# Row means fused on VectorE, squares alone on ScalarE, and a first load in two pieces: a change to a load, compute, store kernel

## The chip, the cores and the metric

The kernel runs on one core of a Trainium2 chip. The metric is the device time of one execution in microseconds (us). "Span" is the time from the first to the last instruction in a profile; it is some 1.8 us shorter than the time. In the views DVE is VectorE, ACT ScalarE, POOL GpSimd and SP SyncE, the engine that issues the DMAs here; a q after a name is that engine's sequencer. A transfer has landed when its completion is signalled. The "chain" is the profile's own account of the work that ended last, followed back from step to step to what released it.

## The reference

```python
x = np.random.randn(1024, 4096).astype(np.float32)     # axis = -1
mean = np.mean(x, axis=axis, keepdims=True)
return ((x - mean) ** 2).astype(np.float32)
```

16.78 MB are read and as many written; per element there is one addition for the mean, one subtraction, one multiplication.

## The kernel before

The 1024 rows are two tiles of 128 partitions with four whole rows (64 KiB) in each partition. A tile is loaded by one DMA, worked on in place, and stored by one DMA, all issued by SP.

```python
for i in range(ntiles):                       # ntiles = 2
    x_tile = io.tile([P, Q * D], F32)         # P = 128, Q = 4, D = 4096
    nc.sync.dma_start(out=x_tile, in_=x_t[i])
...
for i in range(ntiles):
    row = [tiles[i][:, q * D:(q + 1) * D] for q in range(Q)]
    m3 = mean_on_act(row[3])                  # ScalarE: Identity with accumulator
    m0 = mean_on_dve(row[0])                  # VectorE: reduce_sum, then a scaling of 128x1
    square_on_act(row[3], m3)                 # ScalarE: Square with the bias -mean
    m1 = mean_on_dve(row[1]); square_on_act(row[0], m0)
    m2 = mean_on_dve(row[2]); square_on_act(row[1], m1)
    square_on_act(row[2][:, :H], m2)          # H = 2304 of 4096 columns
    back = row[2][:, H:]
    nc.vector.tensor_scalar_add(out=back, in0=back, scalar1=m2)
    nc.vector.tensor_mul(out=back, in0=back, in1=back)
    nc.sync.dma_start(out=out_t[i], in_=tiles[i])
```

Of the kernel before, what the change touches and what calls it, by code (L numbers as in the profile page):

```python
# [2 lines left out]

os.environ.setdefault("NEURON_RT_ULTRASERVER_MODE", "4")

# [4 lines left out]

F32 = mybir.dt.float32
ACT = mybir.ActivationFunctionType


@with_exitstack
def kernel(
    ctx: ExitStack,
    tc: tile.TileContext,
    x: bass.AP,
    axis: bass.AP,  # L20
    out: bass.AP,
):



    nc = tc.nc

    B, D = x.shape
    P = nc.NUM_PARTITIONS
    Q = 4  # L30
    H = D * 9 // 16
    assert B % (P * Q) == 0
    ntiles = B // (P * Q)
    inv_d = 1.0 / float(D)

    x_t = x.rearrange("(n p q) d -> n p (q d)", p=P, q=Q)
    out_t = out.rearrange("(n p q) d -> n p (q d)", p=P, q=Q)

    io = ctx.enter_context(tc.tile_pool(name="io", bufs=ntiles))
    scratch = ctx.enter_context(tc.tile_pool(name="scratch", bufs=1))  # L40
    stats = ctx.enter_context(tc.tile_pool(name="stats", bufs=2 * ntiles * Q))

    tiles = []
    for i in range(ntiles):
        x_tile = io.tile([P, Q * D], F32)
        nc.sync.dma_start(out=x_tile, in_=x_t[i])  # L46
        tiles.append(x_tile)

    inorder = tc.keep_in_program_order

    def mean_on_act(row):
        copy = scratch.tile([P, D], F32)
        neg_mean = stats.tile([P, 1], F32)
        nc.scalar.activation(  # L54
            out=copy, in_=row, func=ACT.Identity, scale=-inv_d, accum_out=neg_mean
        )
        return neg_mean

    def mean_on_dve(row):
        neg_sum = stats.tile([P, 1], F32)  # L60
        neg_mean = stats.tile([P, 1], F32)
        inorder(nc.vector.reduce_sum(  # L62
            out=neg_sum, in_=row, axis=mybir.AxisListType.X, negate=True
        ))
        inorder(nc.vector.tensor_scalar_mul(out=neg_mean, in0=neg_sum, scalar1=inv_d))  # L65
        return neg_mean

    def square_on_act(part, neg_mean):
        inorder(nc.scalar.activation(  # L69
            out=part, in_=part, func=ACT.Square, bias=neg_mean, scale=1.0  # L70
        ))

    for i in range(ntiles):
        row = [tiles[i][:, q * D:(q + 1) * D] for q in range(Q)]
        m3 = mean_on_act(row[3])
        m0 = mean_on_dve(row[0])
        square_on_act(row[3], m3)
        m1 = mean_on_dve(row[1])
        square_on_act(row[0], m0)
        m2 = mean_on_dve(row[2])  # L80
        square_on_act(row[1], m1)
        square_on_act(row[2][:, :H], m2)
        back = row[2][:, H:]
        nc.vector.tensor_scalar_add(out=back, in0=back, scalar1=m2)  # L84
        nc.vector.tensor_mul(out=back, in0=back, in1=back)  # L85
        nc.sync.dma_start(out=out_t[i], in_=tiles[i])


# [1 line left out]
_INS = ['x', 'axis']  # L90
_OUTS = [((1024, 4096), 'float32')]

_NUMBERS = {'axis': -1}


# [26 lines left out]
```

## Time and profile before

| | before |
|---|---|
| time, median of the first 3 runs | 83.25 us (83.16 to 83.27) |
| span of the profiled run | 81.4 us |
| VectorE, ScalarE busy | 33.4 us, 34.7 us |
| DMA packets, share of 16 engines | 96.0% |
| loads landed | 22.71 and 42.05 us |
| stores issued | 39.68 and 58.96 us |

The busy shares alone say which engine has time to spare. What bounds the kernel is read from the windows between the landings and the issues in the last two rows; the prediction below shows those lines. For the experiments one more view is needed: windows of 2 us around the place where the second load ends and the first store begins. Its columns are those of the windows table in the prediction: busy time of VectorE, ScalarE and GpSimd, the clock, the DMA share, GB/s.

```profile
38.00:40.00 2.00, 1.60 (x1) 1.47 (x1) 0.00 (x0) 1.00 1.21 524
40.00:42.00 2.00, 0.00 (x0) 0.00 (x0) 0.00 (x0) 1.00 1.22 524
```

In each of these windows every one of the 16 DMA engines starts one packet of 64 KiB (524 GB/s in 2 us is 16 of them). A packet is booked whole where it starts, so the DMA share times 2 us is the mean duration of a packet: 1.21 x 2 = 2.42 us for the last packets of the second load, 2.44 for the first of the store.

### The profile page before, as it was taken

The numbers are of one execution on the slowest core, as the hardware profiler recorded it, in microseconds if no ns is written. First come the engines' busy times: TensorE is split into PE (matmuls) and PEld (weight loads), VectorE is DVE, ScalarE is ACT, GpSimd is POOL, SyncE is SP. The second block draws the span as 40 slices with busy tenths as digits, with TensorE's granted clock in tenths as the row PEclk, the third lists the DMA queues.
The fourth block names the chain that finished last, engine by engine and source line by source line (L and its number), as shares of the span: only waits on it lengthen the run. The fifth ranks groups of instructions, "written<-read, shape, count | busy, mean of one in ns | idle before, by whom it ended". The sixth has DMA issues, their size and how long they took to land.

```text
span 81.4 us, 79 instructions
## 1 busy us (share of the span) xinstructions
DVE 33.4 (41%) x16; ACT 34.7 (43%) x13; POOL 0.2 (0%) x4
## 2 busy tenths in 40 slices
DVE  0000000000089999999439999999900000000000
ACT  6000000000089999999339999999800000000000
POOL 0000000000000000000000000000000000000000
DMA  9099956999982999992999992999997499998390
GB/s 483 32 515 515 483 258 290 515 515 515 515 386 129 515 515 515 515 451 129 451 515 515 515 483 129 418 515 515 515 515 322 193 515 515 515 515 386 161 483 0
DMA packets 577, 33.55 MB, mean 412 GB/s; under 512 B 65, under 2 KB 65, under 8 KB 65
## 3 DMA queue, kind: packets, MB, share of 16 engines
q1 hardware_dynamic: 576, 33.55, 96.0%
q14 instruction: 1, 0.00, 0.0%
HBM read 16.78 MB, written 16.78 MB: 412 GB/s over the span
## 4 chain that ended last, share of the span: by engine, by line
DMA 50%; DVE 21%; SPq 0%; issue 0%
DMA x_tile<-in_x_dram 50%; DVE neg_sum L62 16%; DVE x_tile L85 2%; DVE x_tile L84 1%; DVE neg_mean L65 1%; SPq L46 0%
## 5 line engine op out<-in xcount | busy, mean ns | idle before, releaser
L62 DVE TENSOR_REDUCE neg_sum<-x_tile 128x1 f32<-128x4096 f32 x6 | 26.5, 4413 | 25.2 <-DMA x_tile<-in_x_dram 25.2
L69 ACT ACTIVATE x_tile<-x_tile,neg_mean 128x4096 f32<-128x4096 f32 (+1 forms) x8 | 26.0, 3323 | 0.1
L54 ACT ACTIVATE copy<-x_tile 128x4096 f32<-128x4096 f32 x2 | 7.2, 3617 | 23.3 <-DMA x_tile<-in_x_dram 23.3
L85 DVE TENSOR_TENSOR x_tile<-x_tile 128x1792 f32<-128x1792 f32 x2 | 4.1, 2026 | 0.1
L84 DVE TENSOR_SCALAR x_tile<-x_tile,neg_mean 128x1792 f32<-128x1792 f32 x2 | 2.3, 1154 | 0.1
L54 ACT ACT_TABLE_LOAD x1 | 1.3, 1283 | 0.7 <-PEq L103 0.7
L65 DVE TENSOR_SCALAR neg_mean<-neg_sum 128x1 f32<-128x1 f32 x6 | 0.9, 154 | 0.2
L54 ACT ACTIVATION_READ_ACCUMULATOR copy<-x_tile 128x1 f32 x2 | 0.4, 187 | 0.0
L103 POOL MEMSET const-bfloat16-1.0<- 128x1 bf16 x1 | 0.1, 101 | 0.0
L103 POOL MEMSET const-uint8-127<- 128x1 uint8 x1 | 0.1, 101 | 0.0
L103 POOL MEMSET const-float32-0.0<- 128x1 f32 x1 | 0.1, 98 | 0.2 <-issue 0.2
L103 POOL MEMSET const-float32-1.0<- 128x1 f32 x1 | 0.1, 98 | 0.0
## 6 DMA issues: line engine op xcount, KB each, us to landing
x_tile<-in_x_dram SPq DMA_DIRECT2D x2, 31.4
out_dram<-x_tile SPq DMA_DIRECT2D x2, 21.7
```

Source lines behind the costliest of these rows:

```text
L54: nc.scalar.activation(out=copy, in_=row, func=ACT.Identity, scale=-inv_d, accum_out=neg_mean)
L62: inorder(nc.vector.reduce_sum(out=neg_sum, in_=row, axis=mybir.AxisListType.X, negate=True))
L65: inorder(nc.vector.tensor_scalar_mul(out=neg_mean, in0=neg_sum, scalar1=inv_d))
L69: inorder(nc.scalar.activation(out=part, in_=part, func=ACT.Square, bias=neg_mean, scale=1.0))
L84: nc.vector.tensor_scalar_add(out=back, in0=back, scalar1=m2)
L85: nc.vector.tensor_mul(out=back, in0=back, in1=back)
L103: nc = _bacc.Bacc("TRN2", target_bir_lowering=False, num_devices=1)
```

## The change

The intent: take both kinds of mean off the two engines' long instructions. One fused VectorE instruction adds the two halves of a row and sums the result, 2048 pairs where there were 4096 elements; ScalarE has no mean to compute any more and squares nearly everything. The first load is cut so that its first 2 KiB per partition are a transfer of their own.

```diff
+ADD = mybir.AluOpType.add
...
-    H = D * 9 // 16
+    HEAD = 512
+    HALF = D // 2
+    LAST = D - D // 8
...
-        nc.sync.dma_start(out=x_tile, in_=x_t[i])
+        cuts = [0, HEAD, Q * D] if i == 0 else [0, Q * D]
+        for lo, hi in zip(cuts, cuts[1:]):
+            nc.sync.dma_start(out=x_tile[:, lo:hi], in_=x_t[i][:, lo:hi])
... (mean_on_act, mean_on_dve, square_on_act and their calls go)
+        for q in range(Q):
+            row = tiles[i][:, q * D:(q + 1) * D]
+            pairs = scratch.tile([P, HALF], F32)
+            neg_mean = stats.tile([P, 1], F32)
+            inorder(nc.vector.tensor_tensor_reduce(
+                out=pairs, in0=row[:, :HALF], in1=row[:, HALF:],
+                scale=-inv_d, scalar=0.0, op0=ADD, op1=ADD, accum_out=neg_mean,
+            ))
+            cut = D if q < Q - 1 else LAST
+            nc.scalar.activation(
+                out=row[:, :cut], in_=row[:, :cut],
+                func=ACT.Square, bias=neg_mean, scale=1.0,
+            )
+            if cut < D:
+                rest = row[:, cut:]
+                nc.vector.tensor_scalar_add(out=rest, in0=rest, scalar1=neg_mean)
+                nc.vector.tensor_mul(out=rest, in0=rest, in1=rest)
```

More of the change, by code (lines that the diff above doesn't have):

```diff
@@ L40 @@
     scratch = ctx.enter_context(tc.tile_pool(name="scratch", bufs=1))
-    stats = ctx.enter_context(tc.tile_pool(name="stats", bufs=2 * ntiles * Q))
+    stats = ctx.enter_context(tc.tile_pool(name="stats", bufs=ntiles * Q))
     tiles = []
@@ L45 @@
         x_tile = io.tile([P, Q * D], F32)
-        nc.sync.dma_start(out=x_tile, in_=x_t[i])
+        cuts = [0, HEAD, Q * D] if i == 0 else [0, Q * D]
+        for lo, hi in zip(cuts, cuts[1:]):
+            nc.sync.dma_start(out=x_tile[:, lo:hi], in_=x_t[i][:, lo:hi])
         tiles.append(x_tile)
     inorder = tc.keep_in_program_order
-    def mean_on_act(row):
-        copy = scratch.tile([P, D], F32)
-        neg_mean = stats.tile([P, 1], F32)
-        nc.scalar.activation(
-            out=copy, in_=row, func=ACT.Identity, scale=-inv_d, accum_out=neg_mean
-        )
-        return neg_mean
@@ L59, in mean_on_dve @@
-    def mean_on_dve(row):
-        neg_sum = stats.tile([P, 1], F32)
-        neg_mean = stats.tile([P, 1], F32)
-        inorder(nc.vector.reduce_sum(
-            out=neg_sum, in_=row, axis=mybir.AxisListType.X, negate=True
-        ))
-        inorder(nc.vector.tensor_scalar_mul(out=neg_mean, in0=neg_sum, scalar1=inv_d))
-        return neg_mean
-    def square_on_act(part, neg_mean):
-        inorder(nc.scalar.activation(
-            out=part, in_=part, func=ACT.Square, bias=neg_mean, scale=1.0
-        ))
@@ L73 @@
-    for i in range(ntiles):
-        row = [tiles[i][:, q * D:(q + 1) * D] for q in range(Q)]
-        m3 = mean_on_act(row[3])
-        m0 = mean_on_dve(row[0])
-        square_on_act(row[3], m3)
-        m1 = mean_on_dve(row[1])
-        square_on_act(row[0], m0)
-        m2 = mean_on_dve(row[2])
-        square_on_act(row[1], m1)
-        square_on_act(row[2][:, :H], m2)
-        back = row[2][:, H:]
-        nc.vector.tensor_scalar_add(out=back, in0=back, scalar1=m2)
-        nc.vector.tensor_mul(out=back, in0=back, in1=back)
+    for i in range(ntiles):
+        for q in range(Q):
[3 more added lines that the diff above has]
+            inorder(nc.vector.tensor_tensor_reduce(
+                out=pairs,
+                in0=row[:, :HALF],
+                in1=row[:, HALF:],
+                scale=-inv_d,
+                scalar=0.0,
+                op0=ADD,
+                op1=ADD,
+                accum_out=neg_mean,
+            ))
+            cut = D if q < Q - 1 else LAST
+            nc.scalar.activation(
+                out=row[:, :cut],
+                in_=row[:, :cut],
+                func=ACT.Square,
+                bias=neg_mean,
+                scale=1.0,
+            )
[3 more added lines that the diff above has]
+                nc.vector.tensor_mul(out=rest, in0=rest, in1=rest)
```

## The prediction

> **What bounds the kernel now.** I read the page of the kernel before first: busy shares, DMA queues, and the chain that ended last.
>
> ```profile
> span 81.4 us, 79 instructions
> ...
> DVE 33.4 (41%) x16; ACT 34.7 (43%) x13; POOL 0.2 (0%) x4
> ...
> q1 hardware_dynamic: 576, 33.55, 96.0%
> ...
> DMA 50%; DVE 21%; SPq 0%; issue 0%
> ```
>
> VectorE and ScalarE work under half of the span; the packets of the one DMA queue fill 96.0% of the time of its 16 engines. The chain seems to say that VectorE still holds 21% of the way to the end, but its shares sum to 71%: it stops where the second store is issued, and says nothing of what that store found in front of it. So I asked for the windows between the four events that the timeline gives: first load landed (22.71), first store issued (39.68), second load landed (42.05), second store issued (58.96).
>
> ```profile
> core 0: us, DVE busy (x) ACT busy (x) POOL busy (x), PEclk, DMA share, GB/s
> 1.70:22.71 21.01, 0.00 (x0) 0.31 (x1) 0.00 (x0) 1.00 1.07 449
> 22.71:39.68 16.97, 16.71 (x8) 16.72 (x6) 0.00 (x0) 1.00 1.00 433
> 39.68:42.05 2.37, 0.00 (x0) 0.00 (x0) 0.00 (x0) 1.00 1.03 442
> 42.05:58.96 16.91, 16.71 (x8) 16.72 (x6) 0.00 (x0) 1.00 1.00 434
> 58.96:80.30 21.34, 0.00 (x0) 0.00 (x0) 0.00 (x0) 1.00 0.91 393
> ```
>
> The column before the last is the DMA share. It is 1.00 in both stretches of computing: the first is covered by the second load, the second by the first store. (A packet is booked whole at its start, which puts the first row above 1 and the last below it.) From 1.75 us, when packets start, to the last window's end the queue hardly rests: 33.55 MB in 78.6 us is 427 GB/s. What is left outside it is 1.7 us of start and 1.1 us of end in the span, and the 1.85 us between the span (81.4) and the time (83.25).
>
> The second thing to know is how much slack the computing has. The issues of the stores give it:
>
> ```profile
> 39.68 19.67 SPq L86 DMA_DIRECT2D out_dram<-x_tile  x2
> ...
> DMA to landing us min/median/max: 21.6/21.7/21.7
> ```
>
> A store alone needs 8.39 MB / 0.433 = 19.4 us, so of its 21.7 us some 2.3 are waiting behind the transfer in front and the latency at both ends. The first load shows a latency: issued at 0.73, its first packets start at 1.75, 1.0 us later. So the first store was issued at most about 1.3 us before it would leave a hole. **Earlier stores gain next to nothing; stores later by over about a microsecond cost one for one.**
>
> The third view is the DMA rows of three zooms of 1 us in 40 slices (from 1.5, from 4.5 and from 7.0 us), which show when each engine's first, second and third packets start:
>
> ```profile
> DMA  0000000000990099099999000000000090000000
> ...
> DMA  0000000009009090900090999900000090000900
> ...
> DMA  0000009090090900990999000000090000900000
> ```
>
> The first mark moves from 1.75 (slice 10 of 25 ns) to 4.72 to 7.15: the first 64 KiB packet takes 3.0 us, later ones 2.4. So the stream pays about 0.6 us once to get going.
>
> **What the Trainium skill says.** First, "DMA: Bandwidth & Descriptors", section "Where 436 GB/s comes from": the ports give 435.2 GB/s. The windows' 433 and 434 agree; this queue has nothing left. Second, "VectorE: DVE Perf Modes", "The perf-mode tier table": tensor_reduce and fp32 tensor_tensor both run at one element a cycle (0.96 GHz). The rows by form agree:
>
> ```profile
> L62 DVE TENSOR_REDUCE neg_sum<-x_tile 128x1 f32<-128x4096 f32 x6 | 26.5, 4413 | 25.2 <-DMA x_tile<-in_x_dram 25.2
> L69 ACT ACTIVATE x_tile<-x_tile,neg_mean 128x4096 f32<-128x4096 f32 x6 | 21.8, 3698 | 0.1
> L69 ACT ACTIVATE x_tile<-x_tile,neg_mean 128x2304 f32<-128x2304 f32 x2 | 4.4, 2200 | 0.0
> L85 DVE TENSOR_TENSOR x_tile<-x_tile 128x1792 f32<-128x1792 f32 x2 | 4.1, 2026 | 0.1
> ```
>
> 4096/0.96 is 4267 ns of the 4413, and 1792/0.96 is 1867 of the 2026: 1 cycle per element and 146 to 159 ns fixed. The page does not list the fused instruction of the change; that it too takes a pair a cycle is my assumption. Third, "ScalarE: Activation LUTs", "What ACT_TABLE_LOAD costs": about 1283 ns plus 1380 of drain. The trace has the 1283 at 0.73 us, where nothing waits for it. Fourth, "DMA: Bandwidth & Descriptors", "Why small descriptors are slow (HBM only)": a fixed cost of a few cycles per packet. No data packet here is small, but the zoom on the end (78 to 81.4 us) has 16 packets of 4 bytes, one per engine, in 0.3% of the time: 10 ns each.
>
> **The change part by part.**
>
> (a) Means. Removed per tile: three reductions of 4413 with their scalings of 154 ns on VectorE, and on ScalarE one mean of 3617 and a read of its accumulator of 187. Added: four fused instructions over pairs, 2048/0.96 + 159 = 2.29 us each (estimated from the tensor_tensor row), each followed by an accumulator read; with the 0.19 of ScalarE's own read, a mean costs about 2.5 us. VectorE falls from 16.7 to about 4 x 2.5 plus the tail of 512 columns: TENSOR_SCALAR over 1792 took 1154 and TENSOR_TENSOR 2026, so 512 take about 0.49 and 0.69 (1.04 and 0.53 ns less per column dropped), 11.2 us in all, and never in the way, because a mean per 2.5 us outruns a square per 3.6.
>
> (b) Squares. Before, three full rows and 2304 columns, 13.01 us in the timeline (their sum 13.29 less three overlaps of 0.093). Now three full rows and 3584 columns. The slope (3698 - 2200)/1792 is 0.836 ns per column, so 3584 take 3270: 3 x 3.698 + 3.270 - 0.28 = 14.08 us. The first must await the first mean.
>
> (c) The stage. 2.5 + 14.1 + 0.1 to the issue = 16.7 us, against 16.97 now: stores leave **0.3 us earlier**. The order of instructions shows one snag: the table load of ScalarE now carries the waits for the first load, so it runs at about 22.7. 1.28 us hide behind the first mean's 2.5; with the page's drain, 2.66, it would delay the first square by 0.2. So the first store is 0.1 to 0.3 earlier, the second 0.3. Both are hidden by the busy queue. I credit 0.05 us for small holes between the second load and the first store.
>
> (d) The first load. Same bytes; each engine gets eight packets of 2 KiB more and one more semaphore packet, at 10 ns each: +0.09 us, on the path, because the queue is the path. Its third issue costs SP another 0.4 us, but the second part is issued by about 1.6 us, while 16 KiB per engine keep the engines busy from 1.75 until well past 2.3 (16 KiB / 27 GB/s = 0.6, plus the 0.6 of start). It may trim the 0.6 us of start if short packets fill the pipe sooner; I credit 0.1.
>
> Sum: 83.25 - 0.05 + 0.09 - 0.1 = **83.2 us**.
>
> **The rivals.**
> 1. The fused instruction runs at half rate. Then a mean takes 2048 x 2/0.96 + 159 + 190 = 4.6 us, the fourth is ready at 18.5 after landing, its square ends at 21.8, and the first store leaves near 44.5, 4.8 later. Less the slack of about 1.3 there is a hole of 3.5 us: about 86.8. The second stage ends at 63.9, near the end of the delayed first store, so it adds little. For it: nothing in this profile shows the instruction. Against it: the running sum is fed by one result per cycle as the reduction before is.
> 2. The chain is right as it reads, and VectorE's 21% are on the path. Then the saving of the second stage, 0.3 us, is had in full: 82.9. Against it: DMA share 1.00 in that window.
> 3. The start is what the split buys: the whole 0.6 us of the first packet goes, 82.7. For it: somebody cut only the first load. Against it: a read must travel to HBM and back whatever its size, so I think most of it stays.
> 4. The small runs are slow: 256 KiB at half rate, and a late second part, +0.6: 83.8.
>
> **Range and chances.** Rivals 2 to 4 span 82.7 to 83.8 and are all within 1%; the repeats spread over 0.11. I take 82.8 to 83.6 for 8 in 10. Faster by 2% (under 81.6) would need 1.65 us out of a queue that has 0.6 to give: 1%. Slower by 2% (over 84.9) is rival 1 or something like it: 5%. Within 2%: 94%.
>
> **What would show it.** Right: VectorE busy about 22 us and ScalarE about 30, the fused row near 2.3 us, stages of about 16.7 us, DMA share 1.00 while they run, stores landing over 21 us after their issue, and the same span to a few tenths. Step (d) is told by the first packets: if second-round starts stay near 4.7 us, the start was not shortened. Wrong: a fused row of over 4 us; a DMA share well below 1 around 40 to 44 us; a store landing in under 20 us, which would mean that it found the queue empty; or a landing of the first load far from 22.7.

## The result and the profile after

The changed kernel takes 83.22 us (median of 6 runs, 83.05 to 83.58), the kernel before 83.23 (6 runs, 83.16 to 83.27): ratio 1.0004, 95% interval 0.9983 to 1.0024. Here and below a ratio is the mean time of one kernel's runs over that of the other's of the same rounds, so it is not quite the ratio of the medians quoted.

The page of the changed kernel, busy times, queue and chain:

```profile
span 81.5 us, 84 instructions
...
DVE 20.8 (25%) x20; ACT 29.4 (36%) x9; POOL 0.2 (0%) x4
...
q1 hardware_dynamic: 720, 33.55, 95.8%
...
DMA 50%; ACT 13%; ACTq 4%; DVE 3%; SPq 1%; issue 0%
```

VectorE lost 12.6 us of work and ScalarE 5.3, and the span did not move. The chain put VectorE at 21% before; it puts ScalarE and its sequencer at 17% now, and the time is the same. Whether such a share is on the path at all is tested below (e3_no_compute, e11_bare_second). The windows with the same borders as those shown of the kernel before tell why:

```profile
22.71:39.68 16.97, 10.38 (x10) 15.36 (x5) 0.00 (x0) 1.00 1.00 433
...
42.05:58.96 16.91, 10.36 (x10) 14.08 (x4) 0.00 (x0) 1.00 1.00 434
```

The DMA share and the GB/s in both stages of computing are to the digit those of before. The rows by form (elements out and in, count, busy us, mean ns) and then the timeline of the first stage show the new work:

```profile
L61 DVE CUSTOM_DVE_ANT_0 pairs<-x_tile 128x2048 f32<-128x2048 f32 x8 | 18.3, 2291 | 31.7 <-DMA x_tile<-in_x_dram 31.5
L72 ACT ACTIVATE x_tile<-x_tile,neg_mean 128x3584 f32<-128x3584 f32 x2 | 6.5, 3265 | 0.0
L61 DVE DVE_READ_ACCUMULATOR2_ANT neg_mean<- 128x1 f32 x8 | 0.7, 81 | 0.0
```

```profile
22.71 1.28 ACT L72 ACT_TABLE_LOAD   x1 [22.71 <-DMA x_tile<-in_x_dram]
22.76 2.29 DVE L61 CUSTOM_DVE_ANT_0 pairs<-x_tile 128x2048 f32<-128x2048 f32 x1 [22.76 <-DMA x_tile<-in_x_dram]
...
25.10 14.08 ACT L72 ACTIVATE x_tile<-x_tile,neg_mean 128x4096 f32<-128x4096 f32 x4 [1.10 <-DVE neg_mean L61]
...
39.20 19.61 SPq L83 DMA_DIRECT2D out_dram<-x_tile  x2
```

The first load lands where it did (22.71), the fused instruction takes 2291 ns for its 2048 pairs, the table load now stands behind the load but ends 1.1 us before the first mean is there, and the first store goes out at 39.20, 0.48 us earlier than before. That gain does not show in the time.

The spread of the changed kernel (0.53 us against 0.11) was not foreseen. It rests on one run of six, 83.58; the other five lie within 0.22. Later, 11 runs of the kernel before spread over 0.36 and over 0.43 us, so that the changed kernel spreads more is not shown.

### The profile page after: what moved, and what is told of

Read it like the earlier page. It is cut to its first block, busy times and chain, and to the rows that moved or that the text cites. A ratio compares the mean times of both kernels' runs of the same rounds, so it can differ in the third digit from the quotient of the medians.

```text
span 81.5 us, 84 instructions
## 1 busy us (share of the span) xinstructions
DVE 20.8 (25%) x20; ACT 29.4 (36%) x9; POOL 0.2 (0%) x4
## 4 chain that ended last, share of the span: by engine, by line
DMA 50%; ACT 13%; ACTq 4%; DVE 3%; SPq 1%; issue 0%
DMA x_tile<-in_x_dram 50%; ACT x_tile L72 13%; ACTq L114 4%; DVE pairs L61 3%; SPq L52 1%; DVE neg_mean L61 0%
## 5 line engine op out<-in xcount | busy, mean ns | idle before, releaser
L72 ACT ACTIVATE x_tile<-x_tile,neg_mean 128x4096 f32<-128x4096 f32 (+1 forms) x8 | 28.2, 3590 | 6.3 <-DVE neg_mean L61 6.3
L61 DVE CUSTOM_DVE_ANT_0 pairs<-x_tile 128x2048 f32<-128x2048 f32 x8 | 18.3, 2291 | 31.7 <-DMA x_tile<-in_x_dram 31.5
L72 ACT ACT_TABLE_LOAD x1 | 1.3, 1283 | 22.7 <-DMA x_tile<-in_x_dram 22.7
L82 DVE TENSOR_TENSOR x_tile<-x_tile 128x512 f32<-128x512 f32 x2 | 1.4, 692 | 0.1
L81 DVE TENSOR_SCALAR x_tile<-x_tile,neg_mean 128x512 f32<-128x512 f32 x2 | 1.0, 488 | 0.1
L61 DVE DVE_READ_ACCUMULATOR2_ANT neg_mean<- 128x1 f32 x8 | 0.7, 81 | 0.0
```

Of the source, the lines that this page charges most:

```text
L61: inorder(nc.vector.tensor_tensor_reduce(out=pairs, in0=row[:, :HALF], in1=row[:, HALF:], scale=-inv_d, scalar=0.0, op0=ADD, op1=ADD, accu ...
L72: nc.scalar.activation(out=row[:, :cut], in_=row[:, :cut], func=ACT.Square, bias=neg_mean, scale=1.0,)
L81: nc.vector.tensor_scalar_add(out=rest, in0=rest, scalar1=neg_mean)
L82: nc.vector.tensor_mul(out=rest, in0=rest, in1=rest)
```

## The experiments

Twelve kernels ran. Kernels are compared only within the same rounds. The kernel before had a median of 83.16 in the first two calls (11 and 7 runs) and of 83.24 in the third (11 runs).

### The parts of the change, one at a time

**e1_means_only**: the changed kernel with the load left whole.

```diff
-        cuts = [0, HEAD, Q * D] if i == 0 else [0, Q * D]
+        cuts = [0, Q * D]
```

> The change without its split of the first load. Theory (the one DMA queue sets the time, both stages of computing lie behind a transfer): stores still issued 0.3 to 0.5 us earlier than before, time 83.2 us, within 0.15 of both kernels; the spread of the runs as before (0.1). Rival (the chain of the kernel before is right, computing in the second stage is on the path): 0.45 us faster than before, 82.8.

Measured: 83.50 us (83.28 to 83.75, 6 runs), ratio 1.0040 (1.0020 to 1.0059). A miss for both theories: the means alone are neither neutral nor a gain but 0.34 us slower, and their spread is 0.47. Its profiled run took 83.28, so the trace shows its best run.

**e2_split_only**: the kernel before with the split of the first load alone.

```diff
-        nc.sync.dma_start(out=x_tile, in_=x_t[i])
+        cuts = [0, 512, Q * D] if i == 0 else [0, Q * D]
+        for lo, hi in zip(cuts, cuts[1:]):
+            nc.sync.dma_start(out=x_tile[:, lo:hi], in_=x_t[i][:, lo:hi])
```

> The kernel before with the first load split into runs of 2 KiB and 62 KiB, nothing else. Theory (the split moves only packets; it adds some 9 ns per extra packet and does not shorten the start): 83.25 to 83.4 us, first load landing within 0.1 us of 22.7. Rival (the split buys the start, and the change then loses it elsewhere): 82.7 to 83.0. If the wider spread of the changed kernel (83.05 to 83.58) belongs to the split, it shows here and not in the run without the split.

Measured: 83.13 us (83.02 to 83.15, 5 runs), ratio 0.9991 (0.9978 to 1.0004). No gain that could be told from none, and a narrow spread (0.13). The median lies 0.12 under the least that was expected: the price of the extra packets does not show in the time.

### Taking the computing away

**e3_no_compute**: the loop over the rows removed; each tile is stored as it was loaded (wrong, and the comparison with the reference says so).

```diff
-        for q in range(Q):
-            ... (all means and squares)
         nc.sync.dma_start(out=out_t[i], in_=tiles[i])
```

> The changed kernel with all computing taken out: each tile is stored as it was loaded (a wrong result on purpose). The first store can then be issued when the first load lands, 16 us earlier than in the changed kernel. Theory (the queue is full from its first packet to its last): the same time to 0.3 us, 82.9 to 83.3, because 33.55 MB still pass at about 430 GB/s. Rival (the chain that ended last is right: computing is 20% of the way to the end): 17 us less, about 66 us.

Measured: 84.39 us (84.22 to 84.63, 5 runs), ratio 1.0151 (1.0130 to 1.0173). The rival that believes the chain is out by 18 us. But my theory missed too: without any computing the kernel is 1.2 us **slower**. The timeline has the issue, and the 2 us windows have the loss (no compute engines worked, so the columns are GpSimd, clock, DMA share and GB/s):

```profile
22.68 20.82 SPq L57 DMA_DIRECT2D out_dram<-x_tile  x2
```

```profile
38.00:40.00 2.00, 0.00 (x0) 1.00 1.85 524
40.00:42.00 2.00, 0.00 (x0) 1.00 0.00 0
```

The same 16 packets start between 38 and 40 us, the last ones of the second load. Their mean duration is 1.85 x 2 = 3.70 us in place of 2.42: each lasts 1.28 us longer, and no store packet starts before 42. The packets before and after them have their usual length. So the loss sits in one place, the load's last packets, and here the store already waited behind them. From this came the new theory: a store issued *too early* costs time.

### The turn from load to store

**e9_early**: the changed kernel with half of the last row given to VectorE, which has time for it. ScalarE, the later of the two, gets done 1.28 us sooner, and the result is right.

```diff
-    LAST = D - D // 8
+    LAST = D // 2
```

> The changed kernel with half of the last row squared by VectorE, not an eighth: ScalarE has 1536 columns less at the end, 1.28 us, and both stores leave at 37.9 in place of 39.2. The run without computing lost 1.2 us: each engine's last packet of the second load took 3.5 to 4.0 us in place of 2.4, with the first store's packets waiting behind it. New theory (a store that stands in the queue before the load's last packets are under way lengthens those): packets of the store arrive near 38.9, while the last load packets start at 38.6 to 39.2, so part or all of the loss: 83.7 to 84.4, last load packets of over 2.6 us on several engines. Old theory (earlier stores are free): 83.2.

Measured: 84.37 us (84.32 to 84.53, 4 runs), ratio 1.0140 (1.0120 to 1.0160). A better balance of the engines costs 1.1 us against the kernel before.

```profile
37.94 20.69 SPq L83 DMA_DIRECT2D out_dram<-x_tile  x2
```

```profile
38.00:40.00 2.00, 0.00 (x0) 0.00 (x0) 0.00 (x0) 1.00 1.61 524
40.00:42.00 2.00, 0.00 (x0) 0.00 (x0) 0.00 (x0) 1.00 0.38 164
```

The load's last packets take 1.61 x 2 = 3.22 us on average, 2.9 to 3.6 by engine in the trace, and only 5 packets (164 GB/s) start in the next 2 us.

**e10_means_full**: the means without the split, as in e1_means_only, and the last row squared by ScalarE to its end, which puts the store back to where it was.

```diff
-    LAST = D - D // 8
+    LAST = D
-        cuts = [0, HEAD, Q * D] if i == 0 else [0, Q * D]
+        cuts = [0, Q * D]
```

> The means alone (no split of the load), with the last row squared by ScalarE to its end: 512 columns more, so the first store leaves at about 39.6, as in the kernel before, in place of 39.2. New theory (the means alone were 0.34 us slower because of their earlier store): 83.1 to 83.25, runs within 0.25 of each other. Rival (something else of the new means costs the 0.34): 83.5 with the wide spread.

Measured: 83.20 us (83.06 to 83.28, 6 runs), ratio 0.9995 (0.9979 to 1.0011). ScalarE does more, the first store leaves at 39.52 in place of 39.19, and the 0.34 us are gone; the spread is 0.22.

**e11_bare_second**: the first tile computed in full, the second not at all (wrong).

```diff
-    LAST = D - D // 8
+    LAST = D
-        for q in range(Q):
+        for q in range(Q if i == 0 else 0):
```

> All computing of the first tile (last row on ScalarE to its end), none of the second tile, which is stored as it was loaded (wrong on purpose): the first store leaves at about 39.6, the second at about 42.1. New theory (only the turn from the second load to the first store matters, and a store behind a store is free): 83.0 to 83.25, that is 1.2 us less than the run without any computing, though it has 17 us more work. Rival (the loss of that run came from a second store queued early): 84.4. Chain of the kernel before (second stage on the path): about 70.

Measured: 83.14 us (83.00 to 83.24, 6 runs), ratio 0.9988 (0.9971 to 1.0004). With the first tile's 17 us of work put back, the kernel is 1.2 us faster than without any.

```profile
39.66 2.71 SPq L83 DMA_DIRECT2D out_dram<-x_tile  x2
```

```profile
38.00:40.00 2.00, 0.00 (x0) 1.64 (x1) 0.00 (x0) 1.00 1.21 524
```

The load's last packets have their usual 2.42 us. This run's second store was issued at 42.0, some 17 us sooner than in the kernel before and 18 before its first packet started (60.3 in the trace), and that cost nothing. Here a store that waited long behind a store was free; one that waited long behind a load (e3_no_compute) cost 1.2 us.

**e12_full_rows**: the changed kernel, split kept, with the last row on ScalarE to its end.

```diff
-    LAST = D - D // 8
+    LAST = D
```

> The changed kernel, split kept, with the last row squared by ScalarE to its end, so both stores leave 0.43 us later, near 39.6: the lucky hour of the kernel before, with the split. New theory: 83.0 to 83.2, like the split alone, runs within 0.2 of each other, and no slower than the kernel before. Old theory (store times do not matter within the slack): no different from the changed kernel, 83.2 with a spread of 0.5.

Measured: 83.13 us (83.06 to 83.20, 6 runs), ratio 0.9986 (0.9970 to 1.0003).

```profile
39.63 19.68 SPq L83 DMA_DIRECT2D out_dram<-x_tile  x2
```

```profile
38.00:40.00 2.00, 0.00 (x0) 1.60 (x1) 0.00 (x0) 1.00 1.21 524
```

The load's last packets are back at 1.21 x 2 = 2.42 us. It is as simple as the change, needs no VectorE tail, and is no slower than the kernel before; that it beats it is not shown, since its interval contains 1. The changed kernel itself did not run in the same call.

### Later stores: how much slack there is

All four of the following keep the rest of the changed kernel. The extra work is one more Square of the last row, into a scratch tile that nobody reads; the results stay right. (The edits also hold the square that was there in program order; those lines are left out below.)

**e7_late_1us**: 1024 columns more, in the first tile.

```diff
+            if q == Q - 1 and i == 0:
+                again = scratch.tile([P, 1024], F32)
+                inorder(nc.scalar.activation(
+                    out=again, in_=row[:, :1024], func=ACT.Square, bias=neg_mean, scale=1.0
+                ))
```

> The changed kernel with one more square of 1024 columns into a scratch tile in the first tile alone, 1.04 us on ScalarE before the first store. Theory: the first store goes out at about 40.25 in place of 39.2; its first packets start 1.0 to 1.6 us later, at 41.25 to 41.8, when the second load's last packets end at 41.0 to 41.5: at the edge of the slack, so +0.1 to +0.5 us, 83.3 to 83.7. Rival (a microsecond and more of slack is left, so it is free): 83.2. Rival (the first stage is fully on the path): +1.04, 84.25.

Measured: 83.41 us (83.36 to 83.56, 5 runs), ratio 1.0032 (1.0018 to 1.0046). The store left at 40.27, 0.59 us after that of the kernel before, and 0.25 us of it show. The edge of the slack lies between these two times.

**e4_late_first**, **e5_late_both**, **e6_late_last**: a whole row more, 3.6 us, in the first tile, in both, in the last.

```diff
-            if q == Q - 1 and i == 0:                 # e7_late_1us
-                again = scratch.tile([P, 1024], F32)
+            if q == Q - 1 and i == 0:                 # e4_late_first
+            if q == Q - 1 and True:                   # e5_late_both
+            if q == Q - 1 and i == ntiles - 1:        # e6_late_last
+                again = scratch.tile([P, D], F32)     # and row[:, :D]
```

> The changed kernel with one more square of a full row into a scratch tile in the first tile alone: 3.6 us more on ScalarE before the first store, which leaves at 42.8. Theory (one full queue with about 1 us of slack): the queue runs dry from about 41.3 to 44.1, a hole of 2.6 to 3.0 us, and the stream pays its start of about 0.6 us again: 85.9 to 86.9. Rival (chain of the kernel before: the first stage is not in it at all): 83.2.

> The same extra square in both tiles. Theory: the first hole moves the end of the first store to about 64, so the second store, issued at 62.1, still queues behind it; the time is that of the run with the extra square in the first tile alone, to 0.3 us (about 86.4), not twice the loss. Rival (stages add): about 89.6.

> The same extra square in the last tile alone. Theory: the second store leaves at 62.1 when the first store's packets end at about 60.8; a hole of about 2.4 to 3.0 us, and perhaps the 0.6 of start: 85.6 to 86.9. Rival (chain of the kernel before, every us of the second stage counts): +3.6, 86.8. It is the pair with the run of both tiles that tells the two apart: here and there the same loss, not its sum.

Measured: 85.58 us (85.50 to 85.63, 4 runs), 85.52 (85.44 to 85.59, 4 runs) and 85.54 (85.45 to 85.92, 5 runs); ratios 1.0291, 1.0285 and 1.0282, each 0.0015 to 0.0017 either way. Twice the extra work costs what it costs once, in either place. The windows show the hole and its absence. First e4_late_first, then e5_late_both, then e6_late_last:

```profile
40.00:42.00 2.00, 0.82 (x3) 2.00 (x1) 0.00 (x0) 1.00 0.00 0
```

```profile
60.00:62.00 2.00, 0.00 (x0) 2.00 (x1) 0.00 (x0) 1.00 1.22 524
```

```profile
60.00:62.00 2.00, 0.50 (x1) 2.00 (x1) 0.00 (x0) 1.00 0.00 0
```

In the first, no data packet starts between 40 and 42 us: the second load ends at 41.1 to 41.5, and the first store's packets start at 43.7. In the third a hole of this kind stands before the second store. (Its profiled run was the slowest of the five, 85.92 us, with its first load ready 0.4 us late; the hole is there all the same.) In the second, where the first store was late as well, the queue still has work at that time, so the second delay is covered. I had expected up to 0.6 us more in the first and third for a new start of the stream, and both came out just under the range. It was not paid: the first store packets after the hole last 1.23 x 2 = 2.46 us (DMA share 1.23 between 42 and 44 us of e4_late_first), not 3. In these runs only the very first load pays that; no run has a hole before a later load.

### The price of small packets

**e8_runs_2k**: the whole first load in runs of 2 KiB, as two transfers of every other slab of 512 columns.

```diff
-        cuts = [0, HEAD, Q * D] if i == 0 else [0, Q * D]
-        ...
+        if i == 0:
+            to = x_tile[:, :].rearrange("p (c s w) -> p s c w", s=2, w=HEAD)
+            of = x_t[i].rearrange("p (c s w) -> p s c w", s=2, w=HEAD)
+            for s in range(2):
+                nc.sync.dma_start(out=to[:, s], in_=of[:, s])
+        else:
+            nc.sync.dma_start(out=x_tile, in_=x_t[i])
```

> The changed kernel with its first load cut wholly into runs of 2 KiB (two transfers, the even and the odd slabs of 512 columns; same bytes): each engine has 256 packets for it in place of 16. Theory (a packet costs its bytes at 27 GB/s plus about 9 ns, on the full queue): 240 x 9 ns = +2.2 us, 85.2 to 85.8 us, the first load landing near 24.9. Rival (small packets cost nothing here, they overlap): 83.2. Rival (runs of 2 KiB go at half the rate): +19 us.

Measured: 85.80 us (85.65 to 85.90, 4 runs), ratio 1.0317 (1.0302 to 1.0332).

```profile
DMA packets 4560, 33.55 MB, mean 399 GB/s; under 512 B 80, under 2 KB 80, under 8 KB 4176
...
25.48 2.29 DVE L65 CUSTOM_DVE_ANT_0 pairs<-x_tile 128x2048 f32<-128x2048 f32 x1 [25.48 <-DMA x_tile<-in_x_dram]
```

The first load is ready at 25.48 in place of 22.76, 2.72 us later. Its first packets start at 2.14 in place of 1.75, which is 0.39 of it; the other 2.33 over 240 more packets per engine make 9.7 ns a packet (24.9 had been expected, without the later start). A second reading leaves the start out: between 14 and 24 us, where only these packets run, the queue moves 387 GB/s, where packets of 64 KiB made 434. A packet of 2 KiB then takes 84.7 ns in place of 75.5, which is 9.2 ns more. The time grew by 2.6 us, so the price is paid nearly in full at the end of the kernel. The runs of one transfer also lie 4 KiB apart; that was not tested apart from their size.

### All of it by the time of the first store

| run | first store issued (us) | time, median (us) |
|---|---|---|
| e3_no_compute | 22.68 | 84.39 |
| e9_early | 37.94 | 84.37 |
| e1_means_only | 39.19 | 83.50 |
| the changed kernel | 39.20 | 83.22 |
| e10_means_full | 39.52 | 83.20 |
| e12_full_rows | 39.63 | 83.13 |
| e2_split_only | 39.64 | 83.13 |
| e11_bare_second | 39.66 | 83.14 |
| the kernel before | 39.68 | 83.16 to 83.25 |
| e7_late_1us | 40.27 | 83.41 |
| e4_late_first | 42.84 | 85.58 |
| e5_late_both | 42.85 | 85.52 |

e6_late_last and e8_runs_2k are left out, since they lose their time elsewhere. The issue times are those of the one profiled run of each. The second load's last packets start at 38.6 to 39.3 us and end at 41.0 to 41.7 in the kernel before. In these runs the store does as well as anywhere between 39.5 and 39.7, when those packets are under way and have at least 1 us to go, and the kernel before stood there already. No run has it between 37.94 and 39.19, or between 39.68 and 40.27, so the edges are not known more closely.

## Why the prediction was right or wrong

The time was right: 83.2 predicted, 83.22 measured, and the reason that carries it, a full DMA queue with both stages of computing behind a transfer, holds: without any computing (e3_no_compute) the kernel gains nothing, and by e4, e5 and e6 a delay counts where it opens a hole, once. Rival 2, that the chain's share of VectorE is on the path, falls with e11_bare_second, which has no second stage at all and the same time. That the number came out to 0.02 us owes something to luck. The prediction's terms of 0.05 to 0.1 are below what its runs can tell apart, and it held every earlier store to be harmless: for e9_early, whose store leaves 1.26 us before that of the changed kernel, the same reasoning would have given 83.2 again, and 84.37 was measured.

Step by step:

- **(a) Means.** The fused instruction was predicted at 2.29 us and took 2291 ns, so the assumption of a pair per cycle holds and rival 1 is out. The accumulator read was over-sized: 81 ns, not 190. From one mean to the next it is 2.34 us (22.76 to 25.10), not 2.5, and VectorE is busy 20.8 us in place of the 22.4 that the step implied. (The two slopes in its bracket, 1.04 and 0.53 ns, stand in the reverse order of the two instructions.)
- **(b) Squares.** 14.08 us predicted and 14.08 measured.
- **(c) The stage.** Predicted 16.7, measured 16.49 (22.71 to 39.20); the stores are 0.48 us earlier, not 0.3. The table load did not delay the first square: it ended at 23.99, and the square began at 25.10 when its mean came.
- **The slack.** The step "Earlier stores gain next to nothing; stores later by over about a microsecond cost one for one" failed in its first half. Earlier stores can cost up to 1.2 us. The changed kernel moved its store from 39.68 to 39.20, towards those times; its median did not suffer, and that its one run of 83.58 comes from there is not shown. The second half is near: from e7_late_1us to e4_late_first the store leaves 2.57 us later and 2.17 are lost. The same step put the slack at "at most about 1.3 us"; e7_late_1us (0.59 later, 0.25 lost) and e4_late_first (3.16 later, 2.42 lost) leave 0.3 to 0.7.
- **"I credit 0.05 us for small holes".** No time shows such a gain. There was a small hole: in the trace of the kernel before the first store's packets start from 41.14 us on, while the first engines were free at 40.99; in the changed kernel both are 41.05. But the load's latest packet ends at 41.67, a store packet starts there at once, and so no time was to be won.
- **(d) The first load.** The sum of +0.09 and -0.1 was nothing, and the split alone is nothing to be told from zero (e2_split_only); the first load lands at 22.71 in both kernels. The packet price of 10 ns was about right (9.2 to 9.7). Whether the start became shorter is told by when the second long packets start: the zoom on 4.5 to 6.5 us in slices of 50 ns, of the kernel before, the changed kernel and e2_split_only.

```profile
DMA  0000909990999000909000000000000000000000
```

```profile
DMA  0000000000000009999999999099000000000000
```

```profile
DMA  0000000000000909999999900009000000000000
```

The first is at 4.70, 5.25 and 5.15 us (to a slice; 4.72 in the finer zoom of the prediction). With the split an engine has had 16 + 62 = 78 KiB by then in place of 64. The 14 KiB more take 0.53 us at 27 GB/s, and the extra small packets 0.08, so a start as long as before would give 4.72 + 0.53 + 0.08 = 5.33. It came 0.1 to 0.2 us sooner. The means over the 16 packets say the same: 5.00, 5.53 and 5.43. So the credit of 0.1 fits, as far as so small a term can be read, and the extra packets took it back. Rival 3 would have the first at 4.7 with the split, and rival 4 the load about 0.6 us late: both fall. (The prediction's own sign, second-round starts near 4.7 us for a start not shortened, left out the 14 KiB.)

What stays open. Why a waiting store lengthens the load's last packets was not found out; shown is only that it does, on all 16 engines, and that a store waiting behind a store does nothing. The profiled runs of the changed kernel and of e1_means_only took 83.27 and 83.28, and their last load packets are nearly normal (DMA share 1.22 in the window from 38 to 40 us); their slowest runs (83.58 and 83.75) were not seen in a trace. That the 0.34 us of e1_means_only are the same effect is argued from e10_means_full. It moves the store, but it also takes the tail of the last row from VectorE; e3_no_compute, which has no such tail and is slow, shows only that the large loss does not need it. And e1_means_only at 83.50 and the changed kernel at 83.22 issue their stores at the same time but ran in different calls; whether the split helps there or the chip differed was not tested.

## What to carry to other kernels

When the one DMA queue is full from its first packet to its last, compute work taken off the engines need not change the time (here VectorE lost 12.6 us of work and ScalarE 5.3 for none), and the chain that ended last cannot be read as a list of gains; look at the DMA share in the windows of computing. Before making a stage shorter, look at which transfer stands in front of the store that it releases: here a store that left 1.7 us sooner than before, behind a load, cost 1.1 us, and one that left 3.2 us later cost 2.4. When two versions cost the same, the issue time of the store is worth tuning on its own, and giving the last piece to the *busier* engine can be the better choice.

## What the Trainium skill lacked or had wrong

- "DMA: Bandwidth & Descriptors", section "Rules for kernel authors", advises to issue a DMA early, so that it overlaps with computing; no page says that a store queued behind a load on the same queue lengthens that load's last packets. Here they went from 2.42 us to 3.22 (store issued at 37.94) and 3.70 (at 22.68), 1.1 to 1.2 us of the whole time; a store behind a store cost nothing.
- The same page's section on small descriptors gives cycles, and its measured table about 10.5 ns a packet as the floor of a 4 KB transfer issued from GpSimd; the price on a full queue is not there. Here it was 9.2 to 9.7 ns per packet of 2 KiB, nearly all of it on the time.
- "VectorE: DVE Perf Modes", section "The perf-mode tier table", does not list the fused add-and-sum instruction: 2291 ns for 2048 fp32 pairs, the same law as the fp32 tensor_tensor here (2291 is 2048/0.96 + 158, and the one over 512 columns took 692, which is 512/0.96 + 159), and 81 ns for reading its accumulator.
- "ScalarE: Activation LUTs", section "What ACT_TABLE_LOAD costs", adds a drain of about 1380 ns to the 1283 of the load. The 1283 are in the trace; the first square began 1.11 us after the load had ended, as soon as its mean was there, so here the drain did not hold it for 1380 ns.
